# Gate products in plain fp32 over four column tiles, and 1/rms columns by transfers, in a RetNet and mLSTM decoder layer

## The chip, the cores and the metric

The kernel runs on one core of a Trainium2 chip. The metric is the time of one execution on the device in microseconds (us); it was run three times, and the median counts. One more execution was recorded by the hardware profiler. PE is TensorE, DVE is VectorE, ACT is ScalarE, POOL is GpSimd, and SP is the engine whose queue issues most transfers.

## What is computed

One decoder layer in fp32 for 1,024 prompt tokens and 8 x 8 sample tokens (1,088 tokens, D = 1,024). The part that matters here:

```python
h = rmsnorm(x, pre_mix_g)              # x * rsqrt(mean(x*x) + EPS) * g
proj = (h @ w_in).astype(f32)          # 4096 columns of q, k, v and gates, then 8 gate columns
...
gates = take(2 * N_ML_HEADS) + b_g     # 4 input-gate and 4 forget-gate columns
i_pre, f_pre = gates[..., :N_ML_HEADS], gates[..., N_ML_HEADS:]
...
ret_out, S_new = retention_chunked(q_r, k_r, v_r, S_ret)
ml_out, C_new, n_new, m_new = mlstm_chunked(q_m, k_m * scale, v_m, i_pre, f_pre, C, n, m)
```

After that come an output projection with a second norm, and a convolutional feed-forward block with two more norms. The logarithms, running sums and maxima of the eight gate columns steer the mLSTM heads.

## The kernel before

Activations lie feature-major: 128 partitions of features, tokens along the row. The 1,088 tokens are four blocks of 272. Projections use fp32r operands in two parts: `split_to` (L145) copies a value rounded to fp32r on ACT (`hi`) and takes the rest on DVE (`lo`). A projection tile is `dense` (L167): 8 k-steps of three products hi·hi, lo·hi, hi·lo of 128 x 128 weights and 272 columns, 24 products to a block and 96 to a tile of 128 output columns. A weight tile of 512 KB is loaded by SP into a staging buffer (tag `wst`, two of them), split, and used from two pairs of `whi` and `wlo`.

The start of the program (L261 to L300) loads x into `xs` (four tiles, one to a block), multiplies by the norm's gain and splits into `h`. The projections use `h` without 1/rms; that factor comes later. `square_sum` and `rstd_block` (L207) make 1/rms as rows: a product with a matrix of ones spreads the sum over all partitions, so that `rb` [128, 1088] holds 1/rms of each token on every partition. Results are multiplied by `rb` when they leave PSUM, or, for q and k of the retention heads, by rotary tables already multiplied by it. The value v is left unscaled; once turned to token-major it takes 1/rms as a column, `rcol` [128, 9], one column to a chunk of 128 tokens and one to the sample tokens (spread over four groups of 32 partitions), on ACT (L612).

`token_norms` (L328) makes `rcol`: eight products of a chunk of `rb` with one column of the identity, a ninth for a spread copy of the sample tokens, and a copy out of PSUM on DVE. In PE's records each of these fp32 products counts twice.

`gate_proj` (L347) makes the eight gate rows. Its weight tile `wg` is 128 columns wide, with the forget gates in columns 0 to 3 and the input gates in 32 to 35. It splits the weights into one operand of hi and lo columns side by side, and for each block runs 8 k-steps of two products (with the hi and the lo part of `h`): 64 products of 272 columns. For each block ACT copies the lower half, DVE adds the upper, and two DVE steps multiply by `rb` into rows of `yT[3]`; the tag of `yT` is that of `xs`, so `yT` takes the place of the loaded tokens. Two ACT steps add the biases. `gate_rows` (L395), a generator that `mix_head` advances between other work, makes of these rows what the mLSTM heads need: an Abs, Exp, Ln and Exp on ACT, row steps and scans on DVE, and at last the transposes into `cols` on PE.

In `mix_head` for the first head, the order is: v of heads 0 and 1 (tiles in8, in9), q (in0, with the 1/rms rows in `pre_norm`), k (in4), `token_norms`, `gate_proj`, five steps of the gate rows, then the swish gates in12 to in15 (`early_gate`, L513: DVE multiplies by `rb` into `z`, ACT takes the sigmoid, DVE multiplies). Then chunks of the retention head run between the projections of the next. Banks of PSUM come from two pools: psA with 2 and psB with 6. in4 and the gates use psA alone; in12 to in15 use psA for blocks 0 and 2 and psB for 1 and 3. in13_2 is tile in13, block 2.

The program is written in this order, but a scheduler with its own timing model puts each engine's instructions in the order in which they are issued, moves projection products ahead as filler, and chooses which buffer a new tile takes. Each engine then runs its list strictly in order.

The sample step of each head (`sample`, L694) already has plain fp32 products in column tiles: L701 writes four groups of 32 PSUM partitions, 128 columns each.

Of the kernel before, what the change touches and what calls it, by code (L numbers as in the profile page):

```python
# [10 lines left out]
F32 = mybir.dt.float32  # L11
F32R = mybir.dt.float32r
BF16 = mybir.dt.bfloat16
AF = mybir.ActivationFunctionType
ALU = mybir.AluOpType
# [81 lines left out]
def hybrid_layer_kernel(ctx: ExitStack, tc: tile.TileContext, a: dict, o: dict):  # L97
# [24 lines left out]
    def qcols(b):  # L122
        return slice(Q * (b % 2), Q * (b % 2) + Q)

    def flat(name, i, **k):

        t = bigp.tile([P, KT * Q], F32, tag=f"f{i}", name=f"{name}{i}")
        return t.rearrange("p (k n) -> p k n", **k) if k else t

    def bank(p, cols, name, rows=P, dt=F32):  # L130
        t = p.tile([P, 512], dt, tag="bank", name=name)
        return t[:rows, :cols]

    def stage_w(src, name):
        st = wp.tile([P, 2 * HB], F32, tag="wst", name=f"st_{name}")[:, :D]
        nc.sync.dma_start(st, src)
        return st
# [7 lines left out]
    def split_to(x, hi, lo, eng=nc.vector, after=None):  # L145
        act, dve = after or (None, None)
        with tc.issue_after(act.ins) if act else nullcontext():
            act = nc.scalar.activation(hi, x, AF.Copy)  # L148
        with tc.issue_after(dve.ins) if dve and eng is nc.vector else nullcontext():
            last["split"] = act, eng.tensor_tensor(lo, x, hi.bitcast(F32), ALU.subtract)  # L150
        return hi, lo
# [158 lines left out]
    def chunk(t, c):  # L310

        if c < NCH:
            return t[:, c * CH:(c + 1) * CH]
        v = t[:, LP - LEAD:]
        return bass.AP(v.tensor, v.offset, [list(v.ap[0]), [TS // G, G], [1, GW]])
# [4 lines left out]
    def spread_copy(t, out):  # L320

        nc.scalar.activation(spread(out), chunk(t, NCH), AF.Copy)
        return out

    def spread_tile(name):
        return m2.tile([P, NB * 129], F32, tag="vx", bufs=1, name=name)

    def token_norms():  # L328
        ps = bank(psB, 9, "rcol")
        rs = spread_copy(rb, spread_tile("sp_rb")[:, :P])  # L330
        for c in range(9):
            nc.tensor.matmul(ps[:, c:c + 1], chunk(rb, c) if c < 8 else rs, ident[:, 0:1], start=True, stop=True)
        nc.vector.tensor_copy(rcol, ps)


    idb = mp.tile([P, P], BF16, name="idb")
# [8 lines left out]
    gates = []  # L345

    def gate_proj():  # L347
        fg = yT[3][32:32 + NH, 0, :]
        ig = yT[3][:NH, 0, :]
        gates.extend([fg, ig])  # L350
        st = stage_w(a["wg"], "gates").rearrange("p (k c) -> p k c", k=KT)
        w = wp.tile([P, D], F32R, tag="whi", name="w_gates").rearrange("p (k c) -> p k c", k=KT)
        split_to(st[:, :, :64], w[:, :, :64], w[:, :, 64:])
        for b in range(4):
            o0, n = BLK[b]
            ps = bank(psA, n, f"gates{b}")
            for k in range(KT):
                for i, x in enumerate(h[b // 2][k // 4]):
                    nc.tensor.matmul(ps, w[:, k, :], x[:, k % 4, qcols(b)], start=k == i == 0,
                                     stop=k == KT - 1 and i == 1)  # L360
            gs = m2.tile([P, Q], F32, tag="sw", name=f"gs{b}")[:64, :n]
            nc.scalar.activation(gs, ps[64:, :], AF.Copy)
            nc.vector.tensor_tensor(gs, gs, ps[:64, :], ALU.add)
            nc.vector.tensor_tensor(fg[:, o0:o0 + n], gs[0:NH, :], rb[0:NH, o0:o0 + n], ALU.mult)
            nc.vector.tensor_tensor(ig[:, o0:o0 + n], gs[32:32 + NH, :], rb[32:32 + NH, o0:o0 + n], ALU.mult)
        nc.scalar.activation(fg, fg, AF.Identity, bias=vec[0:NH, V_BG:V_BG + 1])
        nc.scalar.activation(ig, ig, AF.Identity, bias=vec[0:NH, V_BG + 1:V_BG + 2])

# [172 lines left out]
    def mix_head(hd, ml):  # L541
# [11 lines left out]
        if ml:  # L553
            proj((16 + hd, evac_norm(q, 1.0)))
            proj((20 + hd, evac_norm(k, SCALE)))
            proj((24 + hd, evac_copy(v)))
        else:
            eq, ek = evac_rot(q, f"q{nm}"), evac_rot(k, f"k{nm}")
            if hd == 0:
                proj((0, eq), mid=pre_norm, banks=lambda i, b: psB)  # L560
                proj((NH, ek))
            else:
                proj((hd, eq))
                proj((NH + hd, ek))
            if hd == 0:
                token_norms()
                yT.extend(flat("yT", i, k=2) for i in range(4))
            if hd > 1:
                proj((2 * NH + hd, evac_copy(v)))
            if hd == 0:  # L570
                gate_proj()
                for _ in range(5):
                    next(rows)
                for i in range(NH):
                    proj((12 + i, early_gate(i)), banks=lambda i, b: psB if b % 2 else psA)
                    next(rows)
                    next(wsums)
                log_exp_tables(last["sigmoid"])
                next(rows)
# [893 lines left out]
```

## Time and profile before

| | |
|---|---|
| three runs | 1341.48, 1342.87, 1345.44 us |
| median | 1342.87 us |
| profiled execution, its own time | 1343.25 us |
| its span, first to last instruction | 1341.5 us |
| PE, DVE, ACT, POOL busy | 98%, 74%, 44%, 32% |
| granted PE clock | 0.995 |
| gate products on PE | from 62.07 us to 71.97 us, with 13 projection products between |

The page gives the busy time of each engine, a row of tenths over 40 slices, the chain of work that ended last, and groups of instructions by line. PEld is the weight load of PE, which runs beside the products. Products overlap in their pipeline: one is shown 0.29 us long though the next starts 0.13 us later, so work is measured from start to start. In a row of a timeline stand start, length, engine, line, operation, output <- inputs, sizes and count, and in brackets how long the engine had been idle and what ended that.

### The profile page before, as it was taken

To read this page: it belongs to the slowest core of one execution; us is meant where nothing else is said; L and a number is where in the kernel's file an instruction comes from. 1 tells how busy PE (TensorE), PEld (TensorE's weight loads), DVE (VectorE), ACT (ScalarE), POOL (GpSimd) and SP (SyncE) were. 2 spreads that over 40 slices of the span, in tenths; PEclk is the share of its full clock that TensorE was granted. 3 is DMA by queue.
4 is the path that set the end of the run, shared out by engine and by line. 5 is a ranking of instruction groups with operands and counts; after the bars stand their busy time and mean duration, and the time that the engine had idled before them with its cause. 6 is when DMAs were issued, how large, how long until landed. Compare 5 with 4: busy or idle time off the path is not lost.

```text
span 1341.5 us, 26943 instructions
## 1 busy us (share of the span) xinstructions
PE 1318.0 (98%) x10607; PEld 1304.6 (97%) x10607; DVE 998.1 (74%) x2020; ACT 596.5 (44%) x1125; POOL 433.9 (32%) x565
## 2 busy tenths in 40 slices
PE   9999999999999999999989999999999999999996
PEld 8999999999999999999989999999999999999995
DVE  6878876447566467577799887877878788996677
ACT  7545433313323337355464343443434455453563
POOL 0345441688773000001143212232122205972002
PEclk9999999999999999999999999999999999999998
DMA  6433542576874214224034434333343359533363
GB/s 241 136 117 126 164 154 71 174 233 211 220 178 142 64 50 152 95 71 161 17 124 157 153 120 145 140 134 137 120 145 138 130 185 326 173 94 96 96 217 133
DMA packets 92734, 192.58 MB, mean 144 GB/s; under 512 B 16192, under 2 KB 41408, under 8 KB 92096
## 3 DMA queue, kind: packets, MB, share of 16 engines
q1 hardware_dynamic: 80304, 148.80, 33.2%
q0 software_dynamic: 12160, 41.95, 10.2%
q8 instruction: 83, 1.36, 0.4%
q14 instruction: 43, 0.35, 0.1%
q10 hardware_dynamic: 144, 0.11, 0.0%
HBM read 134.36 MB, written 56.47 MB: 142 GB/s over the span
## 4 chain that ended last, share of the span: by engine, by line
PE 90%; DVE 6%; ACT 1%; issue 1%; DMA 1%; SPq 0%; DVEq 0%; ACTq 0%
PE in L164 26%; PE out L164 7%; PE up_S L1081 6%; PE up_S L1079 6%; PE up_S L1080 6%; PE up_A L1080 5%; PE up_A L1079 4%; PE up_A L1081 4%; PE dn L1290 4%; PE dn L1291 4%; PE dn L1292 4%; PE up_A L1126 1%; PE up_A L1127 1%; PE up_A L1125 1%; DVE rb L1219 1%
## 5 line engine op out<-in xcount | busy, mean ns | idle before, releaser
L164 PE MATMUL in<-hh,wh_in 128*128 128x272 f32 x1024 | 299.0, 294 | 2.1 <-ACT wh_in L148 1.6
L164 PE MATMUL in<-hl,wh_in 128*128 128x272 f32 x1024 | 297.1, 292 | 0.0
L164 PE MATMUL in<-hh,wl_in 128*128 128x272 f32 x1024 | 294.8, 290 | 0.0
L164 PEld LDWEIGHTS in<-hh,wh_in 128*128 128x128 f32 x1024 | 192.4, 188 | 5.8 <-issue 2.3
L164 PEld LDWEIGHTS in<-hh,wl_in 128*128 128x128 f32 x1024 | 192.5, 189 | 0.6 <-issue 0.3
L164 PEld LDWEIGHTS in<-hl,wh_in 128*128 128x128 f32 x1024 | 192.2, 188 | 0.3 <-DVE hl L229 0.2
L148 ACT ACTIVATE wh_up<-st_up 128x1024 fp32r<-128x1024 f32 x84 | 80.4, 959 | 164.1 <-PE up_S L1080 91.3
L1219 DVE TENSOR_TENSOR rb<-rb 128x544 fp32r<-128x544 f32 x78 | 78.0, 1005 | 34.3 <-ACT rb L1218 33.1
L150 DVE TENSOR_TENSOR wl_up<-st_up,wh_up 128x1024 fp32r<-128x1024 f32 x84 | 96.9, 1156 | 8.8 <-ACT wh_up L148 8.8
L1053 DVE TENSOR_TENSOR Uv<-Uv,up_S 128x272 f32<-128x272 f32 (+1 forms) x200 | 66.7, 378 | 46.1 <-PE up_S L1081 46.1
L1111 POOL TENSOR_TENSOR act<-act 128x544 f32<-128x544 f32 x40 | 65.4, 1635 | 64.0 <-DMA bd<-act 49.0
L1239 POOL TENSOR_TENSOR wd<-wd 128x512 f32<-128x512 f32 x44 | 75.1, 1735 | 32.0 <-issue 13.8
L1218 ACT ACTIVATE rb<-rb 128x544 fp32r<-128x544 f32 x78 | 50.5, 650 | 74.8 <-DMA rb<-bd 64.6
L789 POOL TENSOR_TENSOR tab<-tab 128x256 f32<-128x256 f32 x104 | 79.5, 775 | 11.6 <-DMA tab<-in_wu 7.1
L1094 DVE SCALAR_TENSOR_TENSOR c<-Uv,vec,c 128x1024 f32<-128x1024 f32 (+1 forms) x88 | 69.3, 792 | 9.7 <-ACT c L1092 9.7
L1044 POOL MEMSET Ug<- 128x2 f32 x22 | 2.2, 99 | 219.3 <-DMA xr<-in_x 110.1
L1094 DVE SCALAR_TENSOR_TENSOR c<-Ug,vec,c 128x1024 f32<-128x1024 f32 x88 | 68.9, 819 | 0.0
L789 POOL TENSOR_TENSOR wq<-wq 128x256 f32<-128x256 f32 x56 | 52.0, 939 | 46.4 <-DMA wq<-in_wu 44.2
L1092 ACT ACTIVATE c<-Ug,vec 128x1024 f32<-128x1024 f32 (+1 forms) x44 | 34.6, 834 | 52.1 <-DVE Ug L1057 46.9
L789 POOL DMA_DIRECT2D tab<-in_wu x52 | 36.8, 713 | 49.8 <-DVE k_r L508 36.1
L150 DVE TENSOR_TENSOR wl_in<-st_in,wh_in 128x1024 fp32r<-128x1024 f32 (+2 forms) x33 | 41.3, 1251 | 13.1 <-ACT wh_in L148 13.0
L1079 PE MATMUL up_S<-B3h,wh_up 128*128 128x272 f32 x160 | 46.8, 293 | 3.7 <-ACT Uv L1064 3.7
(566 smaller groups left out, 4611.2 us busy)
## 6 DMA issues: line engine op xcount, KB each, us to landing
rb<-bd SPq DMA_DIRECT2D x76, 272.0 KB, 2.8
st_up<-sd SPq DMA_DIRECT2D x40, 512.0 KB, 3.8
bd<-act SPq DMA_DIRECT2D x33, 544.0 KB, 4.4
st_in<-in_wi SPq DMA_DIRECT2D x31, 512.0 KB, 4.3
tab<-in_wu POOLq DMA_DIRECT2D x52, 256.0 KB, 4.7
sd<-tab POOLq DMA_DIRECT2D x26, 512.0 KB, 3.8
st_up<-in_wu SPq DMA_DIRECT2D x24, 512.0 KB, 3.3
wd<-in_wd SPq DMA_DIRECT2D x44, 256.0 KB, 5.0
```

The lines of the kernel that those rows point to most:

```text
L148: act = nc.scalar.activation(hi, x, AF.Copy)
L150: last["split"] = act, eng.tensor_tensor(lo, x, hi.bitcast(F32), ALU.subtract)
L164: nc.tensor.matmul(ps, u[:, k * P:(k + 1) * P], x[b // 2][k // 4][v][:, k % 4, qcols(b)], start=k == term == 0, stop=k == KT - 1 and term ...
L789: last["sums"] = f(*args)
L1053: nc.vector.tensor_tensor(o_, o_ if x is None else c(x), c(ps), ALU.add)
L1079: nc.tensor.matmul(ps, wh[:, c], xh[:, k, n], start=k == 0, stop=False)
L1080: nc.tensor.matmul(ps, wh[:, c], xl[:, k, n], start=False, stop=False)
L1081: nc.tensor.matmul(ps, wl[:, c], xh[:, k, n], start=False, stop=k == 3)
L1094: nc.vector.scalar_tensor_tensor(c, u(i), cw(i), c, ALU.mult, ALU.add)
L1111: (nc.gpsimd if j + 1 < JT else nc.vector).tensor_tensor(o_, x, y, ALU.subtract)
L1219: nc.vector.tensor_tensor(lo, x, hi.bitcast(F32), ALU.subtract)
L1239: nc.gpsimd.tensor_tensor(quad(p, out), quad(p, x), quad(p, y), op)
```

## The change

- **Gates.** `wg` is not split. DVE multiplies its 8 used columns by the norm's gain, in the staging buffer itself, and PE multiplies it with the loaded tokens `xs` in plain fp32: 8 k-steps, and in each of them four products, one to a block. The weights are 32 columns, and block b writes partitions 32b to 32b + 7 of one bank in a column tile of its own. DVE multiplies by `rb` in one step to a block, for both kinds of gate, into rows 0 to 7 of `yT[3]`, and a transfer moves the input gates to partition 32. The forget gates now are at partition 0. `yT` is taken after the gate products, since they read `xs`.
- **1/rms.** `rcol` is made by six transfers: one row of `rb` goes to memory, one transfer reads 1,024 single elements of it back into 8 columns, and four read 32 elements each for the sample tokens.

```diff
+    rbd = dr.tile([1, T], F32, name="rbd")
+
     def token_norms():
-        ps = bank(psB, 9, "rcol")
-        rs = spread_copy(rb, spread_tile("sp_rb")[:, :P])
-        for c in range(9):
-            nc.tensor.matmul(ps[:, c:c + 1], chunk(rb, c) if c < 8 else rs, ident[:, 0:1], start=True, stop=True)
-        nc.vector.tensor_copy(rcol, ps)
+        nc.sync.dma_start(rbd, rb[0:1, :])
+        nc.sync.dma_start(rcol[:, :NCH], rbd[0, :LP].rearrange("(c p) -> p c", p=P))
+        for g in range(G):
+            nc.sync.dma_start(rcol[GW * g:GW * (g + 1), NCH:], rbd[0, LP - LEAD + TS // G * g:][:GW].unsqueeze(1))
...
     def gate_proj():
-        fg = yT[3][32:32 + NH, 0, :]
-        ig = yT[3][:NH, 0, :]
+        w = stage_w(a["wg"], "gates").rearrange("p (k c) -> p k c", k=KT)
+        gain = vec[:, V_PREMIX:V_PREMIX + KT].unsqueeze(2).broadcast_to([P, KT, NH])
+        for c in range(2):
+            nc.vector.tensor_tensor(w[:, :, NH * c:NH * (c + 1)], w[:, :, 32 * c:32 * c + NH], gain, ALU.mult)
+        ps = bank(psA, Q, "gates")
+        for k in range(KT):
+            for b in range(4):
+                nc.tensor.matmul(ps[GW * b:GW * (b + 1), :], w[:, k, :GW], xs[b][:, k, :],
+                                 start=k == 0, stop=k == KT - 1)
+        yT.extend(flat("yT", i, k=2) for i in range(4))
+        both = yT[3][:2 * NH, 0, :]
+        fg, ig = yT[3][:NH, 0, :], yT[3][32:32 + NH, 0, :]
         gates.extend([fg, ig])
-        st = stage_w(a["wg"], "gates").rearrange("p (k c) -> p k c", k=KT)
-        w = wp.tile([P, D], F32R, tag="whi", name="w_gates").rearrange("p (k c) -> p k c", k=KT)
-        split_to(st[:, :, :64], w[:, :, :64], w[:, :, 64:])
         for b in range(4):
             o0, n = BLK[b]
-            ps = bank(psA, n, f"gates{b}")
-            for k in range(KT):
-                for i, x in enumerate(h[b // 2][k // 4]):
-                    nc.tensor.matmul(ps, w[:, k, :], x[:, k % 4, qcols(b)], start=k == i == 0,
-                                     stop=k == KT - 1 and i == 1)
-            gs = m2.tile([P, Q], F32, tag="sw", name=f"gs{b}")[:64, :n]
-            nc.scalar.activation(gs, ps[64:, :], AF.Copy)
-            nc.vector.tensor_tensor(gs, gs, ps[:64, :], ALU.add)
-            nc.vector.tensor_tensor(fg[:, o0:o0 + n], gs[0:NH, :], rb[0:NH, o0:o0 + n], ALU.mult)
-            nc.vector.tensor_tensor(ig[:, o0:o0 + n], gs[32:32 + NH, :], rb[32:32 + NH, o0:o0 + n], ALU.mult)
+            own = slice(GW * b, GW * b + 2 * NH)
+            nc.vector.tensor_tensor(both[:, o0:o0 + n], ps[own, :], rb[own, o0:o0 + n], ALU.mult)
+        nc.sync.dma_start(ig, yT[3][NH:2 * NH, 0, :])
...
             if hd == 0:
                 token_norms()
-                yT.extend(flat("yT", i, k=2) for i in range(4))
```

Since the scheduler makes the order anew, more moves than the diff says. On PE, ahead of the gates, before (in4_3 is the last block of k, `hh` and `hl` are the parts of `h`):

```order
L164 MATMUL in4_3_743<-hh_11_191,wl_in4_647 128x272
L164 MATMUL in4_3_743<-hl_11_192,wh_in4_646 128x272
L332 MATMUL rcol_774<-cst_80,rb_83 128x1 x2
L332 MATMUL rcol_774<-cst_80,sp_rb_775 128x1
L359 MATMUL gates0_796<-hh_00_146,w_gates_793 128x272
L359 MATMUL gates0_796<-hl_00_147,w_gates_793 128x272
L359 MATMUL gates0_796<-hh_00_146,w_gates_793 128x272
```

And now, at the same place (x0 to x3 are the loaded tokens of the four blocks):

```order
L164 MATMUL in12_1_875<-hl_01_149,wh_in12_842 128x272
L164 MATMUL in12_1_875<-hh_01_148,wh_in12_842 128x272
L356 MATMUL gates_785<-x0_102,st_gates_781 32x272
L356 MATMUL gates_785<-x1_103,st_gates_781 32x272
L356 MATMUL gates_785<-x2_104,st_gates_781 32x272
L356 MATMUL gates_785<-x3_105,st_gates_781 32x272
L356 MATMUL gates_785<-x0_102,st_gates_781 32x272
```

16 products of in12_1 that stood between and behind the gates now stand ahead of them, 9 in the place of the first six rcol products and 7 after in4_3. From the last gate product to the first product of in13_2 there are 151 products before and 150 now; to the first of in15_0, 275 and 274.

On SP before, from the gates' weights on (st_in14 is the staging of tile in14):

```order
L136 DMA st_gates_791<-in_wg 128x1024
L136 DMA st_in12_897<-in_wi 128x1024
L136 DMA st_in13_1030<-in_wi 128x1024
L582 DMA sb_r0_1439<-in_sr 128x8x128
L136 DMA st_in14_1160<-in_wi 128x1024
L136 DMA st_in15_1294<-in_wi 128x1024
L136 DMA st_in1_1748<-in_wi 128x1024
```

And now:

```order
L136 DMA st_gates_781<-in_wg 128x1024
L136 DMA st_in12_840<-in_wi 128x1024
L136 DMA st_in13_973<-in_wi 128x1024
L331 DMA rbd_241<-rb_83 1x1088
L582 DMA sb_r0_1382<-in_sr 128x8x128
L332 DMA rcol_240<-rbd_241 128x8x1
L334 DMA rcol_240<-rbd_241 32x1 x4
L136 DMA st_in14_1103<-in_wi 128x1024
L136 DMA st_in15_1237<-in_wi 128x1024
L366 DMA yT3_821<-yT3_821 4x1088
L136 DMA st_in1_1691<-in_wi 128x1024
```

The six transfers of rcol stand ahead of st_in14, and the input gates' transfer right behind st_in15. st_in15 takes the buffer that the gates' weights hold, and so waits for the last gate product.

On ACT now, from the split of in13 to the first sigmoid (L368 is the input gates' bias, L409 the Ln, L411 the Exp that gives the reciprocal):

```order
L148 ACTIVATE wh_in13_975<-st_in13_973 128x1024
L367 ACTIVATE yT3_821<-yT3_821,vec_66 4x1088
L402 ACTIVATE yT2_820<-yT3_821 4x1088
L368 ACTIVATE yT3_821<-yT3_821,vec_66 4x1088
L403 ACTIVATE yT2_820<-yT2_820 4x1088
L409 ACTIVATE yT2_820<-yT2_820 4x1088
L148 ACTIVATE wh_in14_1105<-st_in14_1103 128x1024
L411 ACTIVATE yT3_821<-yT2_820 4x1088
L521 ACT_TABLE_LOAD
L521 ACTIVATE yT0_818<-z_00_871 128x272
```

Before, the two biases came one after the other and the split of in14 stood behind the first two sigmoids; now the Abs stands between the biases and the split of in14 ahead of the last Exp. On DVE the split of in12 has moved ahead of the last rb block, into the place of the gates' split, and the four rescalings of the gates stand behind the split of in13. On POOL the clearing of yT2 (L399) has moved from the start of the list to behind the third fetch of the weight sums. In the up-projection some neighbours of tiles up4 to up6 on DVE, SP and POOL have changed places.

## The prediction

> **What bounds the kernel now.** I read the page first: busy shares, then the chain of work that ended last.
>
> ```profile
> PE 1318.0 (98%) x10607; PEld 1304.6 (97%) x10607; DVE 998.1 (74%) x2020; ACT 596.5 (44%) x1125; POOL 433.9 (32%) x565
> ...
> PE 90%; DVE 6%; ACT 1%; issue 1%; DMA 1%; SPq 0%; DVEq 0%; ACTq 0%
> ```
>
> TensorE (PE) is busy for 98% of the span and makes 90% of the chain. Next, busy time by stretches (the stretch, its length, then PE, PEld, DVE, ACT, POOL), and the longest of PE's own waits:
>
> ```profile
> 50.00:80.00 30.00, 30.00 (x242) 30.00 (x242) 21.03 (x43) 12.49 (x21) 12.38 (x16) 1.00 0.48 158
> 80.00:140.00 60.00, 60.00 (x490) 60.00 (x489) 49.82 (x110) 30.15 (x56) 28.95 (x30) 1.00 0.33 114
> 680.00:1150.00 470.00, 467.74 (x3718) 467.62 (x3719) 390.16 (x663) 207.34 (x281) 136.15 (x214) 1.00 0.45 155
> ```
>
> ```profile
> PE up_S L1079 <- ACT Uv L1064: 3.7, 1, 3.7
> ```
>
> In the stage that changes (50 to 80 us) and in the next one PE is never idle; its longest wait in the whole program is 3.7 us. So a microsecond of PE work taken out here is a microsecond of the end, unless something that follows PE closely turns late. DVE, ACT, POOL and the queues count only where PE would wait for them.
>
> **What leaves PE.** The chain in order of time, from 50 to 80 us, gives start, length and count of the pieces:
>
> ```profile
> 54.27 1.23 PE rcol L332 x12
> 55.50 6.15 PE in L164 x48
> 61.64 0.56 PE rcol L332 x6
> 62.20 4.12 PE gates L359 x32
> 66.33 1.63 PE in L164 x13
> 67.96 4.01 PE gates L359 x32
> 71.97 8.07 PE in L164 x64
> ```
>
> The 64 gate products take 4.12 + 4.01 = 8.13 us, the 9 transposing products of rcol (18 records) 1.23 + 0.56 = 1.79 us. Removed: 9.92 us. The projection products around them come every 8.07 / 64 = 0.126 us; they are only moved.
>
> **What comes to PE.** 8 k-steps of 4 plain fp32 products of 272 columns, each quad spread over four column tiles. The nearest row for plain fp32 is the sum over squares (PE in order of time):
>
> ```profile
> 47.88 0.62 PE L213 MATMUL ssqb_pm<-sums_sb,ones 128*128 128x272 f32 x2
> ...
> 48.46 0.29 PE L164 MATMUL in<-hl,wh_in 128*128 128x272 f32 x1
> ```
>
> One fp32 product is two records, two passes. From 47.88 to 48.46 lie this product and one projection product (left out): 0.58 - 0.126 = 0.454 us, so 0.227 us a pass. One after another, 32 products would take 64 x 0.227 = 14.5 us, more than what is removed. Everything hangs on whether the four tiles run together. The decode step of each head already has plain fp32 products in four column tiles (L701, 16 records of 128 columns); the first fence is its records in short stretches (x is how many are in flight, each is shown about 0.27 long), the second PE around it:
>
> ```profile
> 147.00:147.04 0.04, 0.04 (x4) 1.00 0.00 0
> 147.08:147.12 0.04, 0.04 (x8) 1.00 0.00 0
> 147.18:147.22 0.04, 0.04 (x12) 1.00 0.00 0
> 147.31:147.36 0.05, 0.05 (x12) 1.00 0.00 0
> ```
>
> ```profile
> 146.63 0.39 PE L748 MATMUL o_r<-S_r,q_r 128*128 128x128 f32 x2
> 146.95 0.65 PE L701 MATMUL o_r<-sb_r,qx 128*32 128x128 f32 x16
> 147.53 0.71 PE L712 MATMUL us_r<-sp_r,kz_r 32*128 32x256 f32 x8
> ```
>
> Records join in fours: four from 146.95, eight by 147.08, twelve by 147.18, and the last four by 147.31, when the first have ended; I read starts of 146.95, 147.06, 147.18 and 147.29, so 0.113 us a quad, where one pass of 128 columns by itself costs 0.227 x 128 / 272 = 0.107. Four tiles cost what one costs, plus 0.006. For 272 columns: 16 quads x (0.227 + 0.006) = 3.73 us. Going in: the two passes of L748 end at 146.63 + 0.214 = 146.84, the first quad starts at 146.95, 0.11 lost; coming out, 147.29 + 0.113 = 147.40 against 147.53, 0.13 lost. Added: 3.73 + 0.24 = 3.97 us. Bounds: 3.63 (16 passes and nothing else) and 14.8 (no overlap). I take 3.97, since L701 is the same form with shorter rows.
>
> The Trainium skill (TensorE: Matmul & The Clock Gate, Measured speedup vs the span model) lists less than a full overlap: 2.38 times for three column tiles and 3.07 for four row tiles. As an estimate by 3.07 the products would take 14.5 / 3.07 = 4.7 us and the gain shrink by 0.8; the quads above are closer to four times, so the trace decides.
>
> PE balance: 9.92 - 3.97 = 5.95 us less.
>
> **What must keep up: the gate rows.** Behind the gates stand chains on ACT and DVE that in turn free the accumulators of the next projections. Before, from the timelines of ACT and DVE, and the group of the rescaling:
>
> ```profile
> 73.53 1.20 ACT L366 ACTIVATE yT<-yT,vec 4x1088 f32<-4x1088 f32 x1 [0.17 <-DVE yT L364]
> 77.13 1.11 ACT L402 ACTIVATE yT<-yT 4x1088 f32<-4x1088 f32 x1
> 82.69 1.28 ACT L520 ACT_TABLE_LOAD   x1
> 83.98 0.75 ACT L520 ACTIVATE yT<-z 128x272 f32<-128x272 f32 x2
> 84.64 1.05 ACT L148 ACTIVATE wh_in<-st_in 128x1024 fp32r<-128x1024 f32 x1
> ```
>
> ```profile
> 78.35 0.71 DVE L404 TENSOR_SCALAR yT<-yT 4x1088 f32<-4x1088 f32 x1 [1.01 <-ACT yT L402]
> 79.10 1.28 DVE L406 SCALAR_TENSOR_TENSOR yT<-yT 4x1088 f32<-4x1088 f32 x1
> 84.44 1.34 DVE L521 TENSOR_TENSOR yT<-yT,z 128x272 f32<-128x272 f32 x2 [0.47 <-ACT yT L520]
> 85.71 1.81 DVE L413 TENSOR_TENSOR yT<-yT 4x1088 f32<-4x1088 f32 x1
> 88.59 0.77 DVE L518 TENSOR_TENSOR z<-in,rb 128x272 f32<-128x272 f32 x2
> ```
>
> ```profile
> L364 DVE TENSOR_TENSOR yT<-gs,rb 4x272 f32<-4x272 f32 x4 | 2.1, 516 | 0.1
> ```
>
> z_02, the first half of the 0.77 at 88.59, empties the bank that in13_2 needs. It is done at 89.0, 17.0 us after the gates' end (71.97). PE reaches in13_2 after 151 products, 151 x 0.126 = 19.0 us: 2.0 us to spare. The same count at in15_0 (275 products) leaves 1.6, the least.
>
> After, from the gates' end: four rescalings of 0.52 to 2.2; SP sends the input-gate rows to partition 32, landing d later; ACT's second bias waits for that, and queued behind it on ACT are the Exp, the Ln, the weight copy wh_in14, the reciprocal and the sigmoids; on DVE two row steps, wl_in14 and z_02. Sum: 2.2 + d + 1.20 + 1.11 + 0.1 + 0.71 + 1.28 + 1.11 + 1.05 (wh_in14, now ahead of the sigmoids) + 1.11 + 1.28 + 0.46 + 1.34 + 1.5 + 0.4 = 14.85 + d, against an arrival at 150 x 0.126 = 18.9. For d the nearest rows of the transfers (KB each, us to landing):
>
> ```profile
> st_in<-in_wi SPq DMA_DIRECT2D x9, 512.0 KB, 4.1
> ...
> st_in<-in_wi SPq DMA_DIRECT2D x1, 128.0 KB, 2.8
> ```
>
> ```profile
> sb_m<-in_sn SPq DMA_DIRECT2D x4, 4.0 KB, 6.4
> ```
>
> From 2.8 (smallest of the loads in this part) to 6.4 (1,024 single elements). I take 4.1: four long rows, but queued right behind the 512 KB load of st_in15. Then z_02 is 19.0 after the gates, 2.0 later than before, and and the least slack of 1.6 is overdrawn by 0.4: PE waits about 0.5 us, once, since a wait moves PE back for all later points. With d = 2.8 it waits nothing, with 6.4 about 2.8.
>
> The Trainium skill (DMA: Bandwidth & Descriptors, Anatomy of one DMA — SWDGE (gpsimd) path) gives 2.0 us plus bytes over 436 GB/s, fitted on GpSimd's queue; as an estimate d would be 2.0 and the wait would vanish. No row of this case shows a transfer that short in time, so this stays beside the sum.
>
> **What costs nothing, and its cover.** The 1/rms columns: six transfers on SP behind the last rb. SP is free there, and ACT is the first reader:
>
> ```profile
> 52.72 0.69 SPq L582 DMA_DIRECT2D sb_r<-in_sr  x1
> 64.99 35.76 SPq L136 DMA_DIRECT2D st_in<-in_wi  x4
> ```
>
> ```profile
> 123.69 1.15 ACT L612 ACTIVATE vts<-x_r,rcol 128x128 f32<-128x128 f32 x4
> ```
>
> Row to memory by 57 or so, 6.4 for the single elements (the row above), four more issues: about 66, 57 us ahead of the reader. If that cover were gone, ACT and then PE would wait what is missing. st_in14, queued behind them, left at 64.99 in any case. The gain folded into the weights: two DVE steps of 128x32 that wait for st_gates early on:
>
> ```profile
> 35.32 0.36 SPq L136 DMA_DIRECT2D st_gates<-in_wg  x1
> ```
>
> Landing at 35.32 + 4.1 = 39.4, and DVE gets there at about 38.9: 0.5 of waiting and some 0.4 of work ahead of the first rb, on an engine that PE does not wait for there; POOL's last sum of squares is delayed with it. DVE and ACT lose the four adds and copies of the gates, off the path.
>
> **The sum.** 9.92 - 3.97 - 0.5 = 5.45 us. The profiled execution took 1343.25 us (span 1341.5), 0.38 above the median of 1342.87. So 1343.25 - 5.45 = 1337.8 for that execution, 1337.4 for the median. About 0.3%, 4.0 us, is what a measurement of this kernel can tell from no change.
>
> **The rivals.**
> *The tiles do not overlap* (slower). 14.8 us added against 9.92 removed: +4.9, 1347.8. It decides from an overlap below 14.5 / 9.7 = 1.5 times. Against it: the quads of L701. For it: the rows here are twice as long and four 272-column streams of fp32 are read at once, which no row shows. Chance 0.06.
> *The gate rows come late.* The wait I price at 0.5 becomes 2 to 3.5, by d of 6 or more, or because POOL clears yT2 (now behind its third fetch, and behind the gates) too late for the Abs that writes there. With d = 6.4: 5.95 - 2.8 = 3.15, 1339.7. For it: slack is 1.6 to 2.0 before and the chain has grown by a transfer and a weight copy. Against: the transfer has only four rows. Chance 0.20, no change.
> *Given back later.* The scheduler has also swapped neighbours in the up-projection (DVE, SP, POOL around up4 to up6). One more wait like the 3.7 us above gives 1341.1, no change; that one gone gives 1333.7. Against: hardly any wait of PE there now (467.74 busy of 470). Chances 0.12 and 0.06.
> *My forecast*, 0.56; its own range is 1336 to 1339.
>
> **Chances and range.** Faster: 0.52 of the forecast's 0.56 and the 0.06 make 0.58. Same: 0.04 + 0.19 + 0.11 = 0.34. Slower: 0.06 and 0.01 from each of the two in the middle, 0.08. The range goes from 1333.8 (a wait gone) to 1341.2 (one more wait); outside lie the tiles and the far ends of the others.
>
> **What would show it.** Gates: 16 quads 0.23 apart, about 4 us from the first to the next in12 product; 14 us means the first rival. No rcol product. PE's waits: at most 1 us under z or in13_2, in14 or in15; 2 us or more there, with ACT idle before its second bias, means the second rival. The lead of about 5.5 us that PE has once in15 is done should still stand at 540, 680 and 1150 us; if it shrinks between two of these, the third. The forecast is wrong if the time is above 1339 or below 1336.

## The result, and the profile after

The changed kernel takes 1338.31 us (median of 7 runs, 1337.70 to 1340.45) against 1343.95 us for the kernel before, run beside it: a ratio of 0.996, 95% interval 0.995 to 0.997, or 5.6 us. It is faster by more than 0.3%, inside the predicted range and 0.9 us above the predicted number. The profiled execution took 1338.31 us, its span 1336.5 us, 5.0 less than before. It was run once more beside the last kernels; that ratio stands below.

Busy shares of the kernel after, from the page:

```profile
PE 1311.7 (98%) x10589; PEld 1296.5 (97%) x10589; DVE 991.3 (74%) x2012; ACT 593.1 (44%) x1119; POOL 434.6 (33%) x565
```

PE's busy time is 6.3 us less (1318.0 before); in the second profile of the same kernel, taken beside the last kernels, it is 1313.3, or 4.7 us less, so this difference is known to a microsecond or two. The chain in order of time through the changed stretch, with start, length and count:

```profile
49.94 12.54 PE in L164 x100
62.48 3.80 PE gates L356 x64
66.28 15.79 PE in L164 x124
```

The rcol products are gone and the gate products are one piece of 3.80 us, where 4.12 and 4.01 stood. PE goes from projections to gates to projections without a wait. Now PE's own waits in the whole program (total, times, longest), those over 1 us:

```profile
PE up_S L1079 <- ACT Uv L1064: 3.7, 1, 3.7
PE ssqb_fin L213 <- DVE facc_sq L1306: 2.1, 1, 2.1
PE in L164 <- ACT wh_in L148: 1.6, 2, 1.3
PE yt_m L684 <- DVE on_m L682: 1.3, 4, 0.5
PE warm L159 <- DVE ones L203: 1.1, 1, 1.1
PE u_r L741 <- ACT vts L612: 1.1, 1, 1.1
```

There is no wait for a z of the gate stage. Two of these rows are not in the list of before: yt_m, 1.3 us in four pieces, and u_r waiting 1.05 us for vts. All waits in the list add up to 14.1 us, those of before to 12.8 (yt_r, yt_m1s and a few small ones went). So 6.3 us less work and 1.3 us more waiting make the 5.0 us of the span. The second profile has no row for yt_m and 0.5 us for u_r.

The lead, by how much earlier PE starts the same tile than before, runs so: 5.9 us at 126 us (first u_r), 5.6 at 161, 5.7 at 308 (first o_m), 5.4 at 518 (out), 4.9 at 545 to 660 and 5.1 at 1093 (dn), 5.3 at the start of the last product and 5.0 at its end. What was gained by 126 us is kept but for 0.6 to 0.9.

The gate rows, on ACT and DVE:

```profile
68.25 1.21 ACT L367 ACTIVATE yT<-yT,vec 4x1088 f32<-4x1088 f32 x1 [4.68 <-DVE yT L365]
69.55 1.11 ACT L402 ACTIVATE yT<-yT 4x1088 f32<-4x1088 f32 x1
71.73 1.20 ACT L368 ACTIVATE yT<-yT,vec 4x1088 f32<-4x1088 f32 x1 [1.06 <-DMA yT<-yT]
72.95 1.11 ACT L403 ACTIVATE yT<-yT 4x1088 f32<-4x1088 f32 x1
```

```profile
66.38 1.78 DVE L365 TENSOR_TENSOR yT<-gates,rb 8x272 f32<-8x272 f32 x4 [1.46 <-PE gates L356]
82.99 0.77 DVE L519 TENSOR_TENSOR z<-in,rb 128x272 f32<-128x272 f32 x2
```

The rescalings end at 68.16, the transfer is issued at 68.19 and has landed when ACT starts its second bias at 71.73: 3.5 us. Behind that bias stands the exponential L403. The first z of the pair at 82.99 is done at 83.4, 17.2 us behind the gates' end; PE would come 18.9 behind it.

### The profile page after: what moved, and what is told of

It reads as the page before. It is cut to its first block, busy times and chain, and to the rows that moved or that the text cites. A ratio compares the mean times of both kernels' runs of the same rounds, so it can differ in the third digit from the quotient of the medians.

```text
span 1336.5 us, 26904 instructions
## 1 busy us (share of the span) xinstructions
PE 1311.7 (98%) x10589; PEld 1296.5 (97%) x10589; DVE 991.3 (74%) x2012; ACT 593.1 (44%) x1119; POOL 434.6 (33%) x565
## 4 chain that ended last, share of the span: by engine, by line
PE 86%; DVE 6%; DMA 3%; ACT 2%; issue 2%; SPq 0%; DVEq 0%
PE in L164 26%; PE up_S L1081 6%; PE up_S L1079 6%; PE up_S L1080 6%; PE out L164 5%; PE up_A L1080 5%; PE up_A L1079 4%; PE up_A L1081 4%; PE dn L1290 4%; PE dn L1292 4%; PE dn L1291 4%; PE up_A L1127 1%; PE up_A L1126 1%; PE up_A L1125 1%; DMA rb<-bd 1%
## 5 line engine op out<-in xcount | busy, mean ns | idle before, releaser
L789 POOL TENSOR_TENSOR wq<-wq 128x256 f32<-128x256 f32 x56 | 48.8, 882 | 49.4 <-DMA wq<-in_wu 47.1
L148 ACT ACTIVATE wh_in<-st_in 128x1024 fp32r<-128x1024 f32 (+2 forms) x33 | 34.0, 1029 | 31.0 <-PE in L164 28.4
```

Of the source, the lines that this page charges most:

```text
L789: last["sums"] = f(*args)
```

## The experiments

My theory: the gain is the PE work that is gone, 8.1 us of gate products for 3.8 because the four column tiles run together, and 1.8 us of rcol; everything else is hidden. The rivals: the tiles are not the cause; the gate rows' transfer limits; the lead is given back at other waits. Ratios are to runs of the kernel before on the same chip, with 95% intervals.

### Each part alone

One kernel takes the new `token_norms` and leaves the gates:

```diff
+    rbd = dr.tile([1, T], F32, name="rbd")
...
-        for c in range(9):
-            nc.tensor.matmul(ps[:, c:c + 1], chunk(rb, c) if c < 8 else rs, ident[:, 0:1], start=True, stop=True)
-        nc.vector.tensor_copy(rcol, ps)
+        nc.sync.dma_start(rbd, rb[0:1, :])
+        nc.sync.dma_start(rcol[:, :NCH], rbd[0, :LP].rearrange("(c p) -> p c", p=P))
...
```

> The kernel before with the transfers for rcol alone; the gates stay as they were (64 fp32r products with the hi/lo halves). My theory (the gain is TensorE work that is gone, and nothing else): the two rcol groups of 1.23 and 0.56 us leave TensorE, the transfers land some 50 us ahead of the first reader, so the time falls by 1.8 us to about 1342.1 (ratio 0.9987), and the lead at the first x_r product of the second head is 1.8 us. Rival 'the whole gain comes from what is late at the new xsel and vts wait or from another order of the work': the lead does not match the removed work, the time is as before or differs by some other amount than 1.8. Rival 'transfers in front of st_in hold up the SP queue': a wait for in or wh_in on TensorE between 66 and 82 us that was not there, time 1343 to 1345.

The other is the kernel after with these lines turned round: the new `gate_proj`, and rcol by TensorE.

> The kernel after, but with rcol by TensorE again (transposing products and a copy from PSUM). My theory: the gates' stretch on TensorE stays at 3.8 us against 8.1 before, the gate rows keep up, so the time falls by 4.3 us from before to about 1339.7 (ratio 0.9968); with the kernel that has the transfers alone this adds to the 6.1 of both, less what is given back later. Rival 'the two parts help each other': this part alone gives less than 3 or more than 5.5 us. The wait of u_r for vts behind sel, which cost 1.05 us in the kernel after, should be smaller here, since TensorE runs 1.8 us less ahead: theory 0 to 0.5 us; if it is still 1 us it does not come from the lead.

Transfers alone: 1341.85 us, 0.9985 (0.9972 to 0.9998). Gates alone: 1340.21 us, 0.9974 (0.9961 to 0.9987). Of 1343.95 that is 2.0 and 3.5 us, together 5.5; both parts gave 5.4 in ratio. The parts add up, as far as intervals of about 1.7 us either way can tell. The first agrees with the 1.8 expected, though PE's lead at the first x_r of the second head (118 us) is 1.4 in its profile; where the rest went was not followed. The second is 0.8 short of 4.3, with 4.3 inside its interval. In the chain of the gates alone, rcol is 1.01 + 0.79 us and the gates 3.87; but PE waits 1.4 us for z:

```profile
PE in L164 <- DVE z L518: 1.4, 2, 0.7
...
PE u_r L740 <- ACT vts L611: 0.4, 1, 0.4
```

In that execution ACT's second bias started 5.66 us after the rows' issue (67.83 to 73.49), not 3.5. PE loses more than the 1.4 us of the list: its lead at the first x_r is 1.9 us, where 8.13 - 3.87 = 4.26 us of work are gone, and 2.3 of the 2.4 us that are missing are lost where z is late. A wait is counted from the shown end of the product before, 0.29 us behind its start, though the next could have started 0.13 behind it; so the list gives less than a wait costs. The second rival is real in size, though it did not show in the first profile of the kernel after.

### The order of the tiles

Tile by tile exchanges the two loops:

```diff
-        for k in range(KT):
-            for b in range(4):
+        for b in range(4):
+            for k in range(KT):
```

> The kernel after with the two loops of the gate products exchanged: all eight products of one column tile, then those of the next. The same 32 products, the same tiles, the same sums; but neighbours in the queue now lie in the same tile. My theory (the tiles of neighbouring products run together, and that is what makes plain fp32 cheap): no overlap, 64 passes of 0.227 us, gates about 14.5 us in place of 3.8, the time about 10.7 us above the kernel after, 1349 (ratio to before 1.0037), less what the later gate rows' slack gives. Rival 'the tile mode itself is fast, in whatever order' or 'TensorE reorders or looks ahead across eight products': gates 3.8 us, time 1338.3.

Two tiles in turn:

```diff
-        for k in range(KT):
-            for b in range(4):
+        for k, b in [(k, b) for p in (0, 2) for k in range(KT) for b in (p, p + 1)]:
```

> The kernel after with the gate products ordered so that only two column tiles alternate: tiles 0 and 1 through all eight k, then tiles 2 and 3. From the run tile by tile (64 passes in 12.12 us, 0.189 each) and the kernel after (16 groups of four passes in 3.81 us, 0.238 each). My theory (passes in different tiles run at the same time, as many as there are tiles in the neighbourhood): 32 pairs of 0.19 to 0.24 us, gates 6.1 to 7.6 us, the time 2 to 3.5 us above the kernel after, 1340.5 to 1342. Rival 'the overlap is worth the same for two tiles as for four, since it only hides the change of weights between neighbours': gates near 3.8 to 4.5 us, time 1338.3 to 1339. Rival 'all four tiles must be loaded for any overlap': near 12 us, time 1345.6.

Tile by tile: 1345.6 us, 1.0011 (0.9996 to 1.0027), the change's gain gone. Two tiles: 1340.45 us, 0.9978 (0.9966 to 0.9989). The gates' piece in the chain in order of time, tile by tile and then two tiles:

```profile
62.47 12.12 PE gates L356 x64
```

```profile
62.46 6.58 PE gates L355 x64
```

PE's other products come in the same order, by their names, tile by tile as in the kernel after. So the overlap across tiles is what makes the change pay. How it works shows in the starts of the single passes. The view by stretches, for the gate products alone (the stretch, its length, PE's busy time and in brackets the passes in flight, granted clock, DMA share, GB/s), tile by tile, with two tiles and in the kernel after:

```profile
62.40:65.17 2.77, 2.77 (x12) 1.00 0.57 195
65.17:66.09 0.92, 0.92 (x9) 1.00 0.46 40
```

```profile
62.39:65.16 2.77, 2.77 (x24) 1.00 0.57 195
65.16:66.09 0.93, 0.93 (x18) 1.00 0.10 35
```

```profile
62.40:65.17 2.77, 2.76 (x48) 1.00 0.56 195
```

In the first 2.77 us there are 12 steps, 0.229 us from one to the next behind the first of 0.25, in all three kernels; a step starts one pass tile by tile, two with two tiles, four in the kernel after. In the next 0.92 us there are four steps, and one pass (two with two tiles) is in flight from before; the other eight (sixteen) start two (four) to a step. Tile by tile all 64 passes start in 52 steps: 12 single, 4 pairs, 8 single, 4 pairs, 8 single, 4 pairs, 12 single. The records don't name the tile of a pass, but these counts fit if at each change of tile the last four passes of one (16 to a tile) run beside the first four of the next. With two tiles it is the same with pairs and fours: 28 steps. In the kernel after it is 16 steps.

So a step costs 0.229 us, whether one, two or four tiles take part, and 52, 28 and 16 steps make 11.9, 6.4 and 3.7 of the 12.12, 6.58 and 3.80 us. My figure for a pass, 0.227 us, held; that no pass would overlap tile by tile did not, and of the expectation's rivals the one in which PE looks ahead came true in part, over four passes. If so, "each engine then runs its list strictly in order" is too strong for PE. The 0.189 us in the expectation for two tiles, 12.12 / 64, is a mean over passes alone and in pairs; no pass takes it.

### The gate rows' transfer

One or four stops in DRAM between the two places (shown for four; for one there is a single `igd` and no loop):

```diff
-        nc.sync.dma_start(ig, yT[3][NH:2 * NH, 0, :])
+        igd = [dr.tile([NH, T], F32, name=f"igd{i}") for i in range(4)]
+        nc.sync.dma_start(igd[0], yT[3][NH:2 * NH, 0, :])
+        for i in range(3):
+            nc.sync.dma_start(igd[i + 1], igd[i])
+        nc.sync.dma_start(ig, igd[-1])
```

> The kernel after with the input gate's rows taken to partition 0 by way of one stop in DRAM, two transfers in a row in place of one. In the runs so far the rows landed 3.6, 4.6 and 5.7 us behind the last rescaling, and TensorE waited 0, 0.7 and 1.4 us for z behind them. A transfer from DRAM was issued 2.3 us behind the store that it waits for (rcol's), so one stop adds about 2.3 us or more: landing at 6 to 7 us. My theory (the rows' slack is used up at about 4 us): TensorE waits 1.5 to 3 us for z, of which the later wait of 1.0 us for vts is given back, so the time rises by 0.5 to 2 us to 1339 to 1340.3. Rival 'z waits for ScalarE's and VectorE's other work, not for the rows': no more than 0.7 us of wait, time 1338.3.

> The same with four stops in DRAM, five transfers in a row: landing at 3.6 + 4 x 2.3 = 12.8 us or later. My theory: TensorE waits about 8 to 10 us for z between 66 and 95 us, the wait for vts at 155 us goes, and the time rises by 7 to 9 us to 1345 to 1347, so that the change would be lost. Rival 'z has other limits': under 2 us of wait, time below 1340.

One stop: 1337.69 us, 0.9957 (0.9941 to 0.9973), and no wait for z at all: my expectation fell. ACT in that kernel:

```profile
68.17 1.21 ACT L369 ACTIVATE yT<-yT,vec 4x1088 f32<-4x1088 f32 x1 [4.68 <-DVE yT L365]
69.47 1.11 ACT L404 ACTIVATE yT<-yT 4x1088 f32<-4x1088 f32 x1
70.61 1.11 ACT L405 ACTIVATE yT<-yT 4x1088 f32<-4x1088 f32 x1
73.15 1.20 ACT L370 ACTIVATE yT<-yT,vec 4x1088 f32<-4x1088 f32 x1 [1.43 <-DMA yT<-igd]
```

The rows landed 5.0 us after their issue, but in this kernel the scheduler had put the exponential (L405) ahead of the bias that waits for them. The forget gates' chain no longer stands behind the transfer.

Four stops: 1345.27 us, 1.0003 (0.9992 to 1.0015). The rows landed at 82.35, 14.4 us after the first issue, and the bias held up the table load and the sigmoids of z:

```profile
67.97 5.03 DMA igd<-yT
...
80.48 1.84 DMA yT<-igd
...
82.35 0.03 ACT yT L372
...
83.56 1.28 ACT L525
```

PE waits 2.9 us for z, 1.5 for wl_in and 1.2 for wh_in in this stage, 5.6 us by the list. Its lead shows 8.1: at the first x_r PE is 5.9 us ahead of the kernel before in the kernel after and 2.2 behind here, inside the 8 to 10 expected. A part of that is the clock, granted at 0.88 from 85 to 90 us and at 0.78 from 90 to 95, at and behind the waits of 1.2 and 1.5 us. The exponentials went ahead here too. The whole gain of the change goes with one late landing.

The moved bias tests the order by itself, with the single transfer:

```diff
-        nc.scalar.activation(ig, ig, AF.Identity, bias=vec[0:NH, V_BG + 1:V_BG + 2])
...
-        nc.scalar.activation(e, e, AF.Exp, scale=-1.0)
+        ex = nc.scalar.activation(e, e, AF.Exp, scale=-1.0)
+        with tc.issue_after(ex.ins):
+            nc.scalar.activation(ig, ig, AF.Identity, bias=vec[0:NH, V_BG + 1:V_BG + 2])
```

> The kernel after with one ScalarE instruction moved: the input gate's bias, which waits for the rows' transfer, is put behind the exponential of the forget gate's rows in ScalarE's queue, where it stood in front of it. In the kernel with one stop in DRAM this order came by itself, and a landing 5.0 us behind the last rescaling cost no wait. My theory (what makes the landing matter is that the forget gate's exponential is queued behind the wait): no wait for z in this execution, whatever the landing, up to about 6 us, z of the second head done 1 us or more earlier against the gates' end than in the kernel after (17.1 us), time 1337.5 to 1338.3. Rival 'the transfer is itself on the chain': the wait for z goes with the landing as before, 0.7 at 4.6 us.

1337.02 us, 0.9946 (0.9934 to 0.9959); no wait for z. The rows were there after 3.7 us at most, which costs no wait in the other order either, so this alone doesn't tell. What tells is when z is done: 15.9 us behind the gates' end, against 17.2 in the kernel after at a landing of 3.5, earlier by the 1 us or more that was expected. The kernel after, unchanged, was run beside it:

> The kernel after once more, unchanged, as the measure for the three kernels that run beside it on the same chip. Theory: 1338 us, ratio to before 0.996. What it tells apart: in the profiles so far the input gate's rows landed 3.6 to 5.7 us behind the last rescaling from run to run, with a wait of 0 to 1.4 us for z; if the landing is as scattered here, this execution shows some wait between 0 and 1.4 us, at the same code.

It gave 1336.94 us, 0.9946 (0.9933 to 0.9958). Its profile shows the scatter:

```profile
68.08 0.75 SPq L366 DMA_DIRECT2D yT<-yT  x1
```

```profile
73.36 1.21 ACT L368 ACTIVATE yT<-yT,vec 4x1088 f32<-4x1088 f32 x1 [2.81 <-DMA yT<-yT]
```

```profile
PE in L164 <- DVE z L519: 0.6, 2, 0.3
...
PE u_r L741 <- ACT vts L612: 0.5, 1, 0.5
```

Same code, 5.3 us to landing instead of 3.5, and 0.6 us of wait, in two pieces; PE's lead at the first x_r is 4.7 us instead of 5.9, so they cost 1.2. Over the profiles with the bias ahead of the exponential, landing and wait were 3.5 and 0 (after), 3.6 and 0 (tile by tile), 4.3 and 0.3, 4.5 and 0.7, 4.6 and 0.7, 5.3 and 0.6, 5.7 and 1.4 us (with two tiles in turn ACT came to the bias 2.5 us after the issue, found the rows there, and no z was late). With the exponential ahead of the bias, 5.0 and 0 (one stop), 5.5 and 0 (in the last kernel below). The z of 83.4 us in the kernel after tells the same without the waits: with the bias ahead it is done 17.1 to 17.4 us behind the gates' end at landings up to 3.6 us and 18.7 to 19.4 at 4.3 to 5.7; with the exponential ahead 15.8 to 16.2, at landings up to 5.5. So the wait is real and the order removes it, up to there; the time of the kernel does not show it, since 1.2 us is below what the runs can tell.

### The wait for vts

In the kernel after, vts is queued on ACT behind the copy to `sel`, whose source `xsel` is loaded into the buffer that out_ss is stored from. I took the wait for a cost of the lead: PE is early, the transfers are not. First the copy on GpSimd:

```diff
-        nc.scalar.activation(sel, xsel[:100, :].rearrange("p (j h c) -> p j h c", j=2, h=NH), AF.Copy)
+        nc.gpsimd.tensor_copy(sel, xsel[:100, :].rearrange("p (j h c) -> p j h c", j=2, h=NH))
```

> The kernel after with the copy to sel on GpSimd in place of ScalarE, so that the vts of the second round are no longer queued behind it. My theory: the wait of 1.05 us of u_r for vts goes, the lead there stays 5.9 us, and the time falls by up to 1.0 us to 1337.3 if nothing later takes it back, and by about 0.5 us, 1337.8, if the later losses (lead 4.8 to 5.2 before any such wait) are the same limits as now. Rival 'the wait is of no consequence, the work behind it has another limit': the wait goes and the time stays 1338.3. Rival 'GpSimd is slower at it and releases the sb buffer later': sb_r loads later, and another wait comes up for sb_r in the second round, time 1338.5 to 1340.

On GpSimd: 1338.48 us, 0.996 (0.9946 to 0.9974). The wait for vts is gone, and the last rival of its expectation came true:

```profile
PE o_r L701 <- DMA sb_r<-in_sr: 1.1, 1, 1.1
```

The copy ran at 169.21 behind GpSimd's other work, the buffer came free late, and PE waited as long elsewhere.

Then `sel` loaded directly:

```diff
-        xsel = m2.tile([P, X_N - X_SEL], F32, tag="sb", bufs=1, name="xsel")
-        nc.sync.dma_start(xsel, a["cx"][:, X_SEL:])
...
-        nc.scalar.activation(sel, xsel[:100, :].rearrange("p (j h c) -> p j h c", j=2, h=NH), AF.Copy)
+        nc.gpsimd.dma_start(sel.rearrange("p j h c -> p (j h c)"), a["cx"][:100, X_SEL:])
```

> The kernel after without the buffer xsel: sel is loaded from DRAM by a GpSimd transfer that casts, so the sb buffer goes from the store of out_ss straight to the next load of sb_r, and ScalarE's copy of 1.06 us is gone. It is meant to take away both the wait for vts (1.05 us in the kernel after) and the wait for sb_r (1.1 us) that came in its place when the copy was put on GpSimd. My theory: neither wait is there, TensorE's lead over the kernel before is 5.9 to 6.0 us after the second round, and the time falls by about 1 us to 1337.3 (ratio to before 0.995). Rival 'the lead is taken back later in any case (it is 4.8 to 5.4 us from 480 us on, and the end is bound by other waits)': both waits gone, lead 5.9 at 300 us, and the time 1338.3 as after. Rival 'the cast transfer holds up GpSimd's queue': the wq transfers or the S buffers are late, time above 1338.5.

It took 1339.4 us, 0.9961 (0.9949 to 0.9974). Both waits are gone, but with nothing to wait for, the transfer of 400 KB went out in the opening and the tokens came late:

```profile
2.02 0.72 POOL L373 DMA_DIRECT2D sel<-in_cx  x1
```

```profile
PE in L164 <- ACT hh L228: 2.2, 1, 2.2
```

The next kernel puts a small copy ahead of that transfer, which holds it back, and the last one adds the moved bias:

```diff
+        nc.vector.tensor_copy(sel[0:1, 0, 0, 0:1], negsb[0:1, 0:1])
         nc.gpsimd.dma_start(sel.rearrange("p j h c -> p (j h c)"), a["cx"][:100, X_SEL:])
```

> As the kernel that loads sel by a casting GpSimd transfer, but with the transfer behind a one-element copy that needs negsb, so that it can't run in the opening, where it held the load of the tokens up by 2.2 us (TensorE waited that long for hh). My theory: no wait for hh above 0.3 us, none for vts and none for sb_r, the lead after the second round stays 5.9 us, and the time is about 1 us below the kernel after, 1337.3 (ratio to before 0.995). Rival 'taken back later': lead 5.9 at 300 us, below 5.3 at the end, time as after. Rival 'GpSimd's queue': wq late, time above 1338.5.

> The two last edits together: sel loaded directly, late, and the input gate's bias behind the exponential. My theory: none of the three waits (z, vts, sb_r), lead 5.9 to 6.1 us from 126 us to the end, time 1336.8 to 1337.4 (ratio to before 0.9950), the fastest of all and below the kernel after by about 1 us. Rival 'the lead is bound by something later': the waits gone and the time still 1338.

Direct and late: 1337.29 us, 0.9944 (0.9930 to 0.9957). No wait for hh, vts or sb_r, and the lead is 6.1 us at 518 and 5.7 at the end. From the first u_r (126 us) to 175 us it rises from 4.7 to 5.6, where in the kernel after it falls from 5.9 to 5.5: for PE the wait is gone for good there. With the moved bias as well: 1337.14 us, 0.9945 (0.9931 to 0.9959); none of the three waits, but the profile is that of its longest execution, 1340.34 us, and the lead goes from 5.2 at the first u_r to 3.1 at the end, not the 5.9 to 6.1 expected. Against 0.9946 for the kernel after beside them, neither is faster: a wait of 0.5 to 1 us taken away is not seen in the time. So the rival "bound by something later" can't be told from "too small to see". No version here is measurably better than the kernel after.

Nor is the wait a cost of the lead. Tile by tile, PE runs 2.4 us behind the kernel before at its first u_r and still waits 1.00 us for vts; with four stops, 2.2 behind and 0.93. SP's issues in the kernel before, after, and tile by tile:

```profile
150.17 0.59 SPq L723 DMA_DIRECT2D out_ss<-sb_r  x1
154.05 0.33 SPq L373 DMA_DIRECT2D xsel<-in_cx  x1
```

```profile
144.61 0.65 SPq L723 DMA_DIRECT2D out_ss<-sb_r  x1
149.54 0.33 SPq L374 DMA_DIRECT2D xsel<-in_cx  x1
```

```profile
152.91 0.66 SPq L723 DMA_DIRECT2D out_ss<-sb_r  x1
158.26 0.33 SPq L374 DMA_DIRECT2D xsel<-in_cx  x1
```

From the issue of out_ss to the start of the copy to `sel` (157.41, 154.22, 162.47) it is 7.2, 9.6 and 9.6 us. Over ten profiles with the copy on ACT, a sum of 7.2 to 7.7 goes with no wait (before, transfers alone), 9.0 to 9.2 with 0.24 to 0.45 us, 9.5 to 9.7 with 0.93 to 1.09. So it is the two transfers that take longer, a store and a load one behind the other, in every kernel with the new gates. Why they do stays open: in the kernel after the DMA engines are busy for 0.81 of the store's time, against 0.72 in the kernel before, but tile by tile it is 0.73 and the store is slower still. It wasn't tried to hold the other transfers off.

## Why the prediction was right, and where its steps were off

**What bounds the kernel** held: 5.95 us less PE work was predicted, 9.92 - 3.80 = 6.1 us came, and 5.9 us of lead stood at 126 us (4.7 in the second profile).

**What leaves PE** held: rcol's 1.79 us are gone, and its transfers alone gave 2.0 us (0.3 to 3.8).

**What comes to PE** held in its sum, 3.97 predicted against 3.80 to 3.87 measured, and in its premise. "Four tiles cost what one costs, plus 0.006": the steps are 0.229 us with one tile and with four. The rows it was read from gave 0.227 for a pass and, with the 0.006, 0.233 for a quad. What was too large is the going in and out, 0.24: 16 x 0.229 = 3.66 leaves 0.14 of the 3.80.

Against 64 passes one after another, 64 x 0.229 = 14.7 us, the gain by the four tiles is 14.7 / 3.80 = 3.9 times. The Trainium skill (TensorE: Matmul & The Clock Gate, Measured speedup vs the span model) has 3.07 times for four row tiles and 2.38 for three column tiles. Four column tiles are neither, and gave 3.9 here; three were not run. I set that page aside because the quads seemed closer to four times, and the runs bear the quads out.

**The first rival's price**, 14.8 us on PE and 1347.8 in time, is right for passes that never overlap, but no run shows that. Tile by tile, where 12 of the 64 passes still run beside others, takes 12.12 us, 12.12 - 9.92 = 2.2 more than before by the same sum, and 1345.6 us; that the order decides is shown, and the sign against before is not certain (0.9996 to 1.0027).

**The gate rows** were sized at 0.5 us of wait. The profile of the result showed none: the transfer took 3.5 us and not 4.1, the rescalings 1.78 us and not 2.2, and the product behind the sigmoid (L522) and the scan's step (L414) 0.79 and 1.27 us, not 1.34 and 1.5. In the same code the list shows 0 and 0.6 us, or 0 and 1.2 of lead, and in near copies up to 1.4, or 2.3 of lead; 0.5 lies within that, by the luck of the landing. The reason given, ACT's exponential queued behind the wait, is shown by the two orders. The rival with 2.8 us needed a landing of 6.4 us, which none of the single transfers reached; at 5.7 us, with the gates alone, 2.3 us were already lost, so its chance of 0.20 does not look too high. That "no row of this case shows a transfer that short in time" as 2.0 us is wrong: in the profile before, out_sp (64 KB) has landed after 1.9. For the gate rows no run shows 2.0, only 2.5 at most.

**Given back later** happened in small pieces, 0.6 to 0.9 us of lead in the first profile, by u_r, yt_m and out, and not in the up-projection, where the lead is 4.9 us at 617 and 5.1 at 1093. The busy time from 680 to 1150 us, 467.74 before and 469.82 after, doesn't tell: PE's longest wait, 3.7 us for Uv, reaches into that stretch in the kernel before and lies ahead of it in the kernel after. yt_m's 1.3 us belong to that one execution. In the second profile the lead falls from 5.5 to 4.5 us between 668 and 693 us, and no row of the list is new there. What differs is the clock around that longest wait (after POOL stand the granted clock, the DMA share and GB/s), in the first and the second profile:

```profile
660.00:700.00 40.00, 36.27 (x279) 36.05 (x278) 38.52 (x55) 27.23 (x36) 16.37 (x18) 0.96 0.34 117
```

```profile
660.00:700.00 40.00, 36.27 (x269) 36.05 (x268) 38.08 (x53) 26.79 (x35) 15.89 (x18) 0.91 0.34 110
```

PE is busy as long and gets 10 products fewer through. Nine of the 14 profiles here, that of the kernel before among them, have 0.96 in this stretch and five 0.91, so a lead that shrinks by 1 us here is the execution's and not the kernel's.

The wait of u_r was missed: the step "DVE, ACT, POOL and the queues count only where PE would wait for them" was applied to the stage of the change alone, and not to the two transfers at 145 to 154 us. It was 1.05 us in one execution and 0.5 in the other.

**What costs nothing** held: the first reader of rcol is at 118.50 us, and in neither profile of the kernel after does a row of PE's waits name hh, x or rb.

## What to carry to other kernels

Small products in different column tiles run together where the queue brings different tiles close to each other: here the next tile's passes started four passes early and no more, so loop over the tiles innermost. A group of up to four tiles then costs what one pass costs; a single pass and a quad that the trace already showed, 0.227 and 0.233 us, gave the price to within 0.2 us in all. Read the starts of the records and not only the length of a piece: 12.12 us over 64 passes is a mean that hides two kinds of step. When a transfer enters a chain, look at what is queued behind the instruction that waits for it on its in-order engine; landings of 5.0 to 5.7 us cost nothing with one order and 0.6 to 1.4 us of wait with the other. Such waits cost PE more than their list says, so follow the lead as well. On a kernel that one engine fills to 98%, work removed from that engine came through nearly whole, and waits under 1 us, though the trace shows them plainly, could not be found again in the time.

## What the runs showed of the hardware

- Plain fp32 passes of 272 columns and 32 output columns start 0.229 us one after another, with one, two or four column tiles in the step; fp32r products of 272 columns beside them come every 0.126.
- At a change of column tile, four steps start twice as many passes as the steps around them (from 65.17 us tile by tile), so a tile's passes seem to start up to four passes ahead of their turn.
- A transfer of four rows from SBUF to SBUF (17 KB), issued by SP, was there for its reader after 2.5 us at most in one execution and after 5.7 in another, in nearly the same code.
- A casting GpSimd transfer of 400 KB in the opening went with a delay of 2.2 us of PE's operands, which no other profile here shows above 0.8.
- Around PE's longest wait (3.7 us) the mean granted clock from 660 to 700 us was 0.96 in nine of the 14 profiles, with 277 to 279 products, and 0.91 in five, with 269 to 271; eight products are 1.0 us at 0.126.
- The mean granted clock of the profiled executions lay between 0.993 and 0.995. The 0.002 between them would be 2.7 us of 1340 if all of it were PE's, as large as the waits looked for here.
